# Two transformer layers on one core: the first 512 columns of each stage computed by tokens, between the two norms

## The chip, the core and the metric

The kernel runs on one core of a Trainium2 chip. The core has five engines with instruction queues of their own: TensorE (PE, with its weight loads shown as PEld), VectorE (DVE), ScalarE (ACT), GpSimd (POOL) and SyncE (SP), which here only issues DMAs. The metric is the device time of one launch in microseconds (us), the median of several runs; lower is better.

## The reference, cut to what matters

One sequence of 256 tokens and width 1024 goes through two layers, all in float32. Each layer is a mixer and a product-key expert layer, and each part begins with an RMS norm. Between the layers stands the first layer's final norm.

```
# layer 1
h    = rmsnorm(x, norm_mix_g);  proj = h @ w_in          # 3584 columns
       # retention (4 heads: q, k, v, gate) and differential attention (4 heads: q, k, v)
x    = x + concat([ret_out, diff_out]) @ w_out
x    = x + peer(rmsnorm(x, norm_ffn_g), wq, subkeys, u, v)
x    = rmsnorm(x, final_norm_g)
# layer 2
h    = rmsnorm(x, norm1);       proj = h @ w_in_2
       # gated delta rule (conv of q, k, v; a_gate) and HGRN2 (f, i, q, gate), two mixing gates
x    = x + mix @ w_out_2
x    = x + peer(rmsnorm(x, norm2), w_pq, sub_keys, expert_u, expert_v)
return rmsnorm(x, final_norm)

def peer(xn, wq, subkeys, u, v):     # 128*128 experts, 8 heads, 16 kept per head
    q = (xn @ wq)                    # 2048 columns: 8 heads x 2 halves x 128
    s = q . subkeys;  top 16 of each half, top 16 of their sums, softmax -> g
    act = gelu(u[e] . xn);  return sum(g * act * v[e])
```

## The kernel before

**Stages.** The program has four stages in a row: `mix1`, `Peer` 1, `mix2`, `Peer` 2, and the last norm (`final`). The 256 tokens are two tiles, `tt` = 0 and 1, of 128. Tokens lie on the partitions of `x`; the normed activations lie transposed, features on the partitions, as `xh` and `xl` (the fp32r-rounded value and what is left of it), 8 chunks of 128 features by 256 tokens.

**Weights.** Weights stream through in the order of a plan, 512 KB (128 x 1024 floats) at a time: `_dma` on SP's queue into a ring of three `raw` buffers, then `_conv` splits `raw` into `hi` (ACT, L159) and `lo` (L164, columns shared between DVE and POOL at `lo_cut`), in rings of three each. `prefetch(n)` issues conversions up to n weights ahead of use. `hold`, `homes` and the like don't exist yet.

**Tiles.** A weight of 128 output columns is used by `tile_ch` (L197): 8 chunks x 3 products (hi xh, hi xl, lo xh) = 24 matmuls of 256 tokens; output columns land on partitions, so a consumer that wants tokens there transposes. The results go to two `mm` banks in turn (in mix2 also `wm` banks). Output projections and the expert value rows go the other way: `acc_tile` (L278) keeps a chunk of activations as PE's weights and streams 512 columns of the weight row, into four `y` banks (two token tiles, two halves).

**Expert layer.** `Peer.run` makes 16 query tiles (`hp`, 8 heads x 2 halves); each starts a background `search` (scores, top 16). Then come 128 rows of u (U stage), and 128 rows of v (V stage). All experts are computed densely and the gates multiply them. The last `LAST` = 2 rows of v are held back: `acc_held` does both for token tile 0, then both for token tile 1, so that tile 0's sums are ready early.

**Seams.** After the last held row a norm starts: for each `tt`, `add_half` (L289 or L291) adds `y` to `x`, ACT squares and sums, DVE multiplies by the norm's weight (L370, in `norm_twice` L385 and L389), POOL takes the power -1/2 (L308), DVE builds a scaled identity (`diagonal`, L300), PE multiplies with it (L323, 16 records of 128 x 128 per token tile: transposes and scales), and ACT and DVE write `xh` (L325) and `xl` (L326). In program order both tiles' adds and transposes come first and the next stage's first `tile_ch` after them; this tile needs both token tiles. The first norm (`norm_first`, L342 to L354) needs no add.

**Order.** Each engine runs its queue in order. The queues are filled by a scheduler that simulates the program and by `issue_after`, which keeps one instruction behind another; background generators (`spawn`, `step`, `pass_round`) insert the attention, search and recurrence work between the weight tiles.

**mix1 and mix2.** `mix1` starts with four gate tiles (sigmoid on ACT, product `sg` L866 on DVE), then, per differential head, tiles q, k and v (v is transposed at L702 into `dv`), then retention. Between the gates and the first head the code computes the lambda of the differential attention on DVE (L742, L872, L874) from two small loads, `sub` and `dl`. `mix2` starts with 24 convolution tiles (three steps L1037 and a product L1049 each on DVE), between which `mix2_in_order` places 16 fillers: 8 `a_gate` tiles (L1454) and 8 `f` tiles. The delta rule's first half, `delta(0)`, needs the conv tiles of heads 0 to 3 and runs behind them.

Of the kernel before, what the change touches and what calls it, by code (L numbers as in the profile page):

```python
# [19 lines left out]
P = 128  # L20
# [64 lines left out]
class K:  # L85
    def __init__(self, tc, ins, ctx, plan):
# [16 lines left out]
        self.lo_cut = D  # L103
        self.uid = 0
# [80 lines left out]
    def tile_ch(self, xh=None, xl=None, tag=None):  # L185
# [13 lines left out]
        return ps  # L199

# [92 lines left out]

    def square(self, src, junk, acc):
# [19 lines left out]
    def transposed(self, tt, x, dr):  # L314
# [3 lines left out]
        for c4 in range(2):  # L318
            tag, ps = self.bank([P, 4, P])
            cs = slice(c4 * 4, c4 * 4 + 4)  # L320
            for c in range(4):
                cc = c4 * 4 + c
                nc.tensor.matmul(out=ps[:, c, :], lhsT=x[:, cc * P:(cc + 1) * P], rhs=dr, start=True, stop=True)  # L323
            h = self.xh[:, cs, ts]
            last = nc.scalar.activation(out=h, in_=ps, func=ACTF.Copy)  # L325
            nc.vector.tensor_tensor(out=self.xl[:, cs, ts], in0=ps, in1=h.bitcast(F32), op=ALU.subtract)  # L326
            self.done(tag)
        self.last_act = last.ins

    def prefetch_behind(self, ahead=3):  # L330

        with self.tc.issue_after(self.last_act):
            self.prefetch(ahead)

    def norm_first(self, g, xn):

        nc = self.nc
        banks = [self.bank([P, 2, 2, P]) for c2 in range(4)]
        for tt in range(2):
            x, s = self.x[:, tt, :], self.columns()  # L340
            self.square(x[:, 512:D], xn[tt][:, 512:D], s[0])
            nc.vector.scalar_tensor_tensor(out=xn[tt][:, 0:512], in0=x[:, 0:512], scalar=1.0 / D, in1=x[:, 0:512],  # L342
                                           op0=ALU.mult, op1=ALU.mult, accum_out=s[1])
            nc.vector.tensor_scalar(out=s[4], in0=s[0], scalar1=s[1], scalar2=EPS, op0=ALU.add, op1=ALU.add)
            self.rsqrt(s[6], s[4])
            dr = xn[tt][:, 0:P]
            self.diagonal(dr, s[6])
            for c in range(NC):
                nc.tensor.matmul(out=banks[c // 2][1][:, c % 2, tt, :], lhsT=x[:, c * P:(c + 1) * P], rhs=dr, start=True, stop=True)
        for c in range(NC):  # L350
            tag, ps = banks[c // 2]
            v, h = ps[:, c % 2].rearrange("p a b -> p (a b)"), self.xh[:, c, :]
            last = nc.scalar.activation(out=h, in_=v, func=ACTF.Copy, scale=g[:, c:c + 1])
            nc.vector.scalar_tensor_tensor(out=self.xl[:, c, :], in0=v, scalar=g[:, c:c + 1], in1=h.bitcast(F32),  # L354
                                           op0=ALU.mult, op1=ALU.subtract)
            if c % 2:
                self.done(tag)
# [555 lines left out]
H = 8  # L913
# [760 lines left out]
```

## Time and profile before

| | |
|---|---|
| time before, median of 3 runs | 2219.83 us (2218.16 to 2219.92) |
| the profiled execution | 2218.6 us |
| its span, first to last instruction | 2216.8 us |
| mean granted TensorE clock | 0.996 |
| PE busy | 2167.8 us, 98% |
| DVE, ACT, POOL busy | 1533.0, 1154.8, 813.5 us |

The span is 1.8 us shorter than the execution's own time. PE is busy in 98% of the span, so all idle time of PE together is 49 us (2216.8 less 2167.8). Rows begin with the start in us from the span's start, then the duration; "[2.38 <-DVE sg L866]" means that the engine stood idle for 2.38 us ahead of the instruction and that VectorE's instruction of line 866 ended this.

### The profile page before, as it was taken

Reading aid. Unit: us, or ns where it says so; the run is one execution under the profiler, and the core shown is the slowest. Engines: PE = TensorE matmul, PEld = TensorE weight load, DVE = VectorE, ACT = ScalarE, POOL = GpSimd, SP = SyncE. Lnnn points to the kernel's source line nnn. Section 1 sums busy time; section 2 is a strip of 40 time slices with the busy share of each in tenths; the row PEclk is TensorE's granted clock in tenths of the full one; section 3 lists DMA queues with packets and bytes.
Section 4 is the critical chain, followed back from the end, with each engine's and each line's share of the span. In section 5 each row is a group of like instructions: output and inputs, shape, how many; then the busy total and the mean of one; then the engine's idle time right before and its main releaser. Section 6 shows DMA issues by size and latency. Waiting matters only on the chain. (4 is left out here: it accounts for less than half of the span.)

```text
span 2216.8 us, 41395 instructions
## 1 busy us (share of the span) xinstructions
PE 2167.8 (98%) x15512; PEld 2016.0 (91%) x15512; DVE 1533.0 (69%) x3122; ACT 1154.8 (52%) x2183; POOL 813.5 (37%) x623
## 2 busy tenths in 40 slices
PE   8999999999999999989999999999999999999998
PEld 8989999999988888879899998999999999888887
DVE  5669986898644544477687787799778885444444
ACT  5645545444455555556455655455454445555554
POOL 3454000000065666646275675620000002665664
PEclk9999999999999999999999999999999999999999
DMA  5555655555556656534444244555555555665654
GB/s 188 155 176 162 185 170 167 157 162 161 172 190 207 200 192 196 193 118 137 131 123 135 68 143 152 173 162 185 178 162 158 157 160 183 193 206 190 195 194 152
DMA packets 103880, 370.89 MB, mean 167 GB/s; under 512 B 12928, under 2 KB 14080, under 8 KB 103424
## 3 DMA queue, kind: packets, MB, share of 16 engines
q1 hardware_dynamic: 101808, 365.21, 52.1%
q10 hardware_dynamic: 1872, 3.04, 0.5%
q8 instruction: 122, 2.00, 0.4%
q14 instruction: 78, 0.64, 0.1%
HBM read 367.16 MB, written 1.05 MB: 166 GB/s over the span
## 5 line engine op out<-in xcount | busy, mean ns | idle before, releaser
L164 POOL TENSOR_TENSOR lo<-raw,hi 128x384 fp32r<-128x384 f32 (+1 forms) x428 | 689.5, 1612 | 1309.1 <-ACT hi L159 1271.4
L159 ACT ACTIVATE hi<-raw 128x1024 fp32r<-128x1024 f32 x684 | 724.0, 1060 | 680.2 <-PE mm L197 403.4
L164 DVE TENSOR_TENSOR lo<-raw,hi 128x640 fp32r<-128x640 f32 (+1 forms) x654 | 668.0, 1022 | 313.5 <-ACT hi L159 306.2
L197 PE MATMUL mm<-xh,hi 128*128 128x256 f32 x2848 | 820.9, 288 | 4.4 <-DVE sg L866 2.9
L197 PE MATMUL mm<-xh,lo 128*128 128x256 f32 x2848 | 807.5, 284 | 0.3 <-DVE lo L164 0.2
L197 PE MATMUL mm<-xl,hi 128*128 128x256 f32 x2848 | 803.9, 282 | 0.9 <-DVE xl L326 0.7
L197 PEld LDWEIGHTS mm<-xh,hi 128*128 128x128 f32 x2848 | 538.2, 189 | 5.9 <-DVE sg L866 3.3
L197 PEld LDWEIGHTS mm<-xl,hi 128*128 128x128 f32 x2848 | 538.9, 189 | 1.8 <-DVE xl L326 1.1
L197 PEld LDWEIGHTS mm<-xh,lo 128*128 128x128 f32 x2848 | 534.8, 188 | 0.7 <-DVE lo L164 0.7
L278 PE MATMUL y<-lo,ah 128*128 128x512 f32 x1024 | 398.2, 389 | 0.0
L278 PE MATMUL y<-hi,ah 128*128 128x512 f32 x1024 | 397.4, 389 | 0.0
L278 PE MATMUL y<-hi,al 128*128 128x512 f32 x1024 | 275.9, 389 | 0.0
L635 DVE TENSOR_TENSOR al<-a,ah 128x256 fp32r<-128x256 f32 x256 | 118.1, 462 | 193.2 <-PE y L278 192.9
L278 PEld LDWEIGHTS y<-hi,al 128*128 128x128 f32 x1024 | 192.2, 188 | 39.9
L278 PEld LDWEIGHTS y<-lo,ah 128*128 128x128 f32 x1024 | 192.3, 188 | 39.8
L278 PEld LDWEIGHTS y<-hi,ah 128*128 128x128 f32 x1024 | 192.2, 188 | 39.8
L634 ACT ACTIVATE ah<-a 128x256 fp32r<-128x256 f32 x256 | 106.5, 417 | 168.3 <-PE y L278 166.7
L197 PE MATMUL wm<-xh,hi 128*128 128x256 f32 x320 | 92.1, 289 | 5.4 <-ACT sq L1059 2.1
L197 PE MATMUL wm<-xh,lo 128*128 128x256 f32 x320 | 90.6, 285 | 0.6 <-DVE lo L164 0.6
L197 PE MATMUL wm<-xl,hi 128*128 128x256 f32 x320 | 90.5, 283 | 0.3 <-DVE xl L326 0.3
L535 DVE TENSOR_TENSOR ow<-ow,w 128x1024 f16<-128x1024 f16 x128 | 87.1, 683 | 0.1
L563 ACT ACTIVATE a<-mm 128x256 f32<-128x256 f32 (+33 forms) x228 | 69.0, 302 | 0.0
(513 smaller groups left out, 2271.6 us busy)
## 6 DMA issues: line engine op xcount, KB each, us to landing
raw<-in_u_dram SPq DMA_DIRECT2D x256, 512.0 KB, 3.5
raw<-in_v_dram SPq DMA_DIRECT2D x256, 512.0 KB, 4.2
raw<-in_w_in_dram SPq DMA_DIRECT2D x108, 512.0 KB, 3.5
raw<-in_wq_dram SPq DMA_DIRECT2D x32, 512.0 KB, 3.7
raw<-in_w_out_dram SPq DMA_DIRECT2D x16, 512.0 KB, 3.6
raw<-in_w_branch_a_dram SPq DMA_DIRECT2D x8, 512.0 KB, 3.5
raw<-in_w_branch_b_dram SPq DMA_DIRECT2D x8, 512.0 KB, 3.6
skT<-in_sk_dram ACTq DMA_DIRECT2D x2, 1024.0 KB, 5.1
```

What stands on the lines that cost most here:

```text
L159: self.nc.scalar.activation(out=h, in_=r, func=ACTF.Copy)
L164: eng.tensor_tensor(out=l[:, a:b], in0=r[:, a:b], in1=h[:, a:b].bitcast(F32), op=ALU.subtract)
L197: self.nc.tensor.matmul(out=ps, lhsT=a[:, c, :], rhs=b, start=(c == 0 and k == 0), stop=(c == NC - 1 and k == 2))
L278: i = self.nc.tensor.matmul(out=self.y[tt][dh], lhsT=p[:, ts], rhs=q[:, ds], start=(first and m == 0), stop=(last and m == 2))
L535: nc.vector.tensor_tensor(out=ow[q], in0=ow[0], in1=some(self.w[:, q]), op=ALU.mult)
L563: nc.scalar.activation(out=a[:, s, n:T], in_=ps[:, n:T], func=ACTF.Gelu)
L634: nc.scalar.activation(out=h, in_=a, func=ACTF.Copy)
L635: nc.vector.tensor_tensor(out=l, in0=a, in1=h.bitcast(F32), op=ALU.subtract)
```

## The change

It has six parts.

1. **By tokens.** `tile_tok` and `seam` are new. The first 512 columns of each stage (mix1: the values of the four differential heads; both expert layers: queries hp 0 to 3; mix2: the first four `a_gate` heads) are no longer four `tile_ch` of 24 matmuls x 256, but 48 matmuls that stream 512 columns, 24 per token tile. Four weights in a new layout (`_quads`) hold them, each 2 chunks x 512 columns. In `seam`, three of four weights are used for tile 0 right after tile 0's transposes, ahead of tile 1's transposes (in mix1 two of them).
2. **Norm order.** `turn` and `behind` keep tile 1's first half of adds behind tile 0's scaled identity, and its second half behind tile 0's last `xl`. `xh` and `xl` are written in pairs of chunks from two banks in turn.
3. **Held rows.** `LAST` goes from 2 to 3. In the V stage a1's space is freed at n = 66, and the v rows converted from there on get homes of their own (`hold`, ring of four); `out_proj` and mix2's output do the same for their last weights, with deeper `prefetch`.
4. **mix1.** Values come token-major as `vt`: no v tile and no L702 transposes in `diff`. The lambda work moves into a generator behind the fourth gate.
5. **mix2.** Four a_gate fillers are gone, two fillers stand among the first 14 conv tiles (before: four among the first 12), then one behind each. `delta(0)` multiplies by the token-major gate `sgt` ahead of its transposes, and takes two banks at once.
6. **Expert layers.** The queries of hp 0 to 3 come from `qt` by two transposes each (8 per layer) and start at hp = 4, 7, 10, 13.

```
+    def tile_tok(self, tt, w, n, y):
+        h, l = w
+        ts = slice(tt * P, (tt + 1) * P)
+        todo = [(x, b, c2) for x, bs in ((self.xh, (h, l)), (self.xl, (h,))) for c2 in range(2) for b in bs]
+        for m, (x, b, c2) in enumerate(todo):
+            self.last_mm = self.nc.tensor.matmul(out=y, lhsT=x[:, 2 * n + c2, ts], rhs=b[:, c2 * 512:c2 * 512 + 512],
+                                                 start=(n == 0 and m == 0), stop=(n == 3 and m == len(todo) - 1)).ins
+
+    def seam(self, norms, before=3):
+
+        self.prefetch(2)
+        norms[0]()
+        with self.tc.issue_after(self.behind[0]):
+            self.prefetch(3)
+        ws = [self.weights() for _ in range(3)]
+        self.quads = [self.bank([P, 512])]
+        for n in range(3):
+            if n == before:
+                norms[1]()
+            self.tile_tok(0, ws[n], n, self.quads[0][1])
+        if before == 3:
+            norms[1]()
+        self.quads.append(self.bank([P, 512]))
+        for n in range(3):
+            self.tile_tok(1, ws[n], n, self.quads[1][1])
+            with self.tc.issue_after(self.last_act):
+                self.prefetch(n + 1)
+        w = self.weights()
+        for tt in range(2):
+            self.tile_tok(tt, w, 3, self.quads[tt][1])
...
+    def turn(self, tt, n):
+
+        return self.tc.issue_after(self.behind[n]) if tt else self.tc.issue_after(self.first_half) if n else nullcontext()
...
-            self.add_half(tt, dh, None)
-            self.square(x[:, hs], xn[:, hs], s[dh])
-        for dh in range(2):
-            hs = self.half(dh)
-            nc.vector.tensor_tensor(out=xg[:, hs], in0=x[:, hs], in1=gn[:, hs], op=ALU.mult)
+            with self.turn(tt, dh):
+                self.add_half(tt, dh, None)
+                self.square(x[:, hs], xn[:, hs], s[dh])
+                self.first_half = nc.vector.tensor_tensor(out=xg[:, hs], in0=x[:, hs], in1=gn[:, hs], op=ALU.mult).ins
...
-LAST = 2
+LAST = 3
...
-            for hp in range(16):
+            for hp in range(4, 16):
                 ps = k.tile_ch()
-                for gen in k.bg[:3]:
-                    pass
+                if hp % 3 == 1:
+                    k.spawn(search(hp // 3 - 1))
                 k.spawn(search(hp, ps))
...
+                    home = lambda: [end.tile([P, D], FR, name=t, tag=t, bufs=4) for t in ("wh", "wl")]
+                    k.hold(k.n_cv - k.n_use, [home] * (P - n - k.n_cv + k.n_use))
...
-                k.prefetch()
...
+                k.prefetch(2 if n < P - 20 else 3 if n < P - LAST - 1 else LAST + 2)
...
-    rest = [("a", h, 0) for h in range(H)] + [("f", h, 0) for h in range(H)]
+    rest = [("a", h, 0) for h in range(4, H)] + [("f", h, 0) for h in range(H)]
     for n, c in enumerate(conv):
         yield c
-        if n % 3 == 2 or n >= 12:
+        if n in (4, 9) or n >= 14:
             yield rest.pop(0)
```

What the scheduler makes of it shows in the engines' queues. First DVE at the start of mix1, before: `lo` is the weights' split, `sg` the gate product, L742 to L874 the lambda work (`sub`, `dl`).

```order
L164 TENSOR_TENSOR lo<-raw,hi 128x640 x3
L866 TENSOR_TENSOR sg<-mm,sig 128x256 x2
L164 TENSOR_TENSOR lo<-raw,hi 128x640
L742 TENSOR_SCALAR sub<-sub 128x1
L872 TENSOR_TENSOR pr<-dl 128x128
L874 TENSOR_REDUCE lam<-pr 128x2
L164 TENSOR_TENSOR lo<-raw,hi 128x640
L866 TENSOR_TENSOR sg<-mm,sig 128x256 x2
```

And DVE at the same place after the change (L167 is the split, L937 the gate product, L951 to L953 the lambda work):

```order
L167 TENSOR_TENSOR lo<-raw,hi 128x640 x5
L937 TENSOR_TENSOR sg<-mm,sig 128x256
L167 TENSOR_TENSOR lo<-raw,hi 128x640
L937 TENSOR_TENSOR sg<-mm,sig 128x256
L167 TENSOR_TENSOR lo<-raw,hi 128x640
L937 TENSOR_TENSOR sg<-mm,sig 128x256
L167 TENSOR_TENSOR lo<-raw,hi 128x640
L937 TENSOR_TENSOR sg<-mm,sig 128x256
L951 TENSOR_TENSOR pr<-dl 128x128
L953 TENSOR_SCALAR sub<-sub 128x1
L952 TENSOR_REDUCE lam<-pr 128x2
```

The three lambda instructions stood ahead of the third gate product, and now stand behind the fourth. Next DVE between `Peer` 1 and mix2, before: L291 adds, L385 and L389 multiply by two norm weights, L390 to L392 are small columns.

```order
L291 SCALAR_TENSOR_TENSOR x<-y,x 128x512 x2
L385 TENSOR_TENSOR a_4058<-x,a_4058 128x512
L389 TENSOR_TENSOR a_4058<-x,a_4058 128x512
...
L291 SCALAR_TENSOR_TENSOR x<-y,x 128x512
L390 TENSOR_SCALAR nrm<-nrm 128x1
...
L391 SCALAR_TENSOR_TENSOR nrm<-nrm 128x1
```

The same place after the change (L332 add, L433 and L435 the products, L345 the scaled identity, L375 `xl`):

```order
L435 TENSOR_TENSOR x_9411<-x,g_9408 128x512
L436 TENSOR_SCALAR nrm<-nrm 128x1
L437 SCALAR_TENSOR_TENSOR nrm<-nrm 128x1
L438 TENSOR_TENSOR nrm<-nrm 128x1
L345 TENSOR_SCALAR x_9412<-k_ident,nrm 128x128
L167 TENSOR_TENSOR lo<-raw,hi 128x640
L332 SCALAR_TENSOR_TENSOR x<-y,x 128x512
L433 TENSOR_TENSOR x_9413<-x,g_9406 128x512
L435 TENSOR_TENSOR x_9414<-x,g_9408 128x512
L375 TENSOR_TENSOR xl<-bg_10855,xh 128x2x128
```

Tile 0's chain down to its scaled identity has no instruction of tile 1 in it any more; one weight split stands between it and tile 1's first add. Last, PE at the same seam, before (L278 a held row, L323 transposes, L197 the first `tile_ch`):

```order
L278 MATMUL y<-hi,al 128x512
L323 MATMUL bg_10923<-a_4058 128x128 x4
L323 MATMUL bg_10930<-a_4058 128x128 x4
L323 MATMUL by_10953<-a_4058 128x128 x4
L323 MATMUL by_10960<-a_4058 128x128 x4
L197 MATMUL wm<-xh,hi 128x256
```

And after the change (L319 a held row, L370 transposes, L216 `tile_tok`):

```order
L319 MATMUL y<-wh,ow_10767 128x512
L370 MATMUL bg_10855<-x_9412,x_9411 128x128 x4
L370 MATMUL bg_10864<-x_9412,x_9411 128x128 x4
L216 MATMUL by_10880<-hi,xh 128x512
L216 MATMUL by_10880<-lo,xh 128x512
...
L216 MATMUL by_10880<-hi,xl 128x512 x2
L370 MATMUL by_10915<-x_9415,x_9414 128x128 x4
L370 MATMUL bg_10924<-x_9415,x_9414 128x128 x4
L216 MATMUL bg_10937<-hi,xh 128x512
```

Between the two tiles' transposes, which stood back to back, 18 matmuls of 512 columns now lie.

## Rows read from the trace of the kernel before

**Rows 1.** Of the page, part 1: each engine's busy time, share, instructions

```profile
PE 2167.8 (98%) x15512; PEld 2016.0 (91%) x15512; DVE 1533.0 (69%) x3122; ACT 1154.8 (52%) x2183; POOL 813.5 (37%) x623
```

**Rows 2.** The timeline at the start; columns: start, duration (both us), engine, line, operation

```profile
6.74 6.62 PE L349 MATMUL by<-xn,x 128*128 128x128 f32 x32 [6.74 <-DVE xn L300]
13.12 0.37 PE L197 MATMUL mm<-xh,hi 128*128 128x256 f32 x1
...
20.29 0.39 PE L197 MATMUL mm<-xh,hi 128*128 128x256 f32 x1 [0.55 <-DVE sg L866]
...
28.68 0.38 PE L197 MATMUL mm<-xh,hi 128*128 128x256 f32 x1 [2.38 <-DVE sg L866]
```

**Rows 3.** The timeline of DVE at the start

```profile
25.38 0.15 DVE L742 TENSOR_SCALAR sub<-sub 128x1 f32<-128x1 f32 x1 [2.28 <-DMA sub<-in_diff_subln_g_dram]
26.95 0.29 DVE L872 TENSOR_TENSOR pr<-dl 128x128 f32<-128x128 f32 x1 [1.41 <-DMA dl<-in_diff_lambda_dram]
```

**Rows 4.** Windows: us, busy time (x records) by engine, granted clock (PEclk), DMA share

```profile
29.00:33.00 4.00, 4.00 (x24) 4.00 (x23) 1.00 (x3) 1.06 (x1) 1.65 (x1) 0.59 0.56 195
955.00:957.00 2.00, 0.00 (x0) 0.00 (x0) 1.96 (x7) 1.31 (x4) 0.08 (x1) 0.50 0.00 0
974.00:984.00 10.00, 6.54 (x48) 5.56 (x48) 8.37 (x27) 6.77 (x20) 4.81 (x3) 1.00 0.34 109
1054.00:1064.00 10.00, 10.00 (x84) 9.81 (x83) 9.90 (x27) 6.36 (x17) 3.11 (x3) 1.00 0.69 200
```

**Rows 5.** The timeline of the first seam, mix1 to Peer 1

```profile
136.80 1.07 POOL L164 TENSOR_TENSOR lo<-raw,hi 128x384 fp32r<-128x384 f32 x1
...
136.93 1.63 DVE L164 TENSOR_TENSOR lo<-raw,hi 128x640 fp32r<-128x640 f32 x1
...
138.48 1.28 DVE L289 TENSOR_TENSOR x<-y,x 128x512 f32<-128x512 f32 x2
...
140.38 0.39 PE L278 MATMUL y<-hi,cl 128*128 128x512 f32 x1
...
143.22 2.02 PE L323 MATMUL bg<-xn,xg 128*128 128x128 f32 x16 [2.45 <-DVE xn L300]
...
147.55 0.39 PE L197 MATMUL mm<-xl,hi 128*128 128x256 f32 x1 [0.34 <-DVE xl L326]
...
147.78 0.28 PE L197 MATMUL mm<-xh,lo 128*128 128x256 f32 x1
...
150.65 0.29 PE L197 MATMUL mm<-xh,lo 128*128 128x256 f32 x1
```

**Rows 6.** The timeline of the second seam, Peer 1 to mix2

```profile
949.17 1.29 DVE L291 SCALAR_TENSOR_TENSOR x<-y,x 128x512 f32<-128x512 f32 x2 [0.30 <-PE y L278]
...
951.01 0.39 PE L278 MATMUL y<-lo,ah 128*128 128x512 f32 x1
...
951.69 0.39 PE L278 MATMUL y<-lo,ah 128*128 128x512 f32 x1
...
951.91 0.39 PE L278 MATMUL y<-hi,al 128*128 128x512 f32 x1
...
957.89 3.76 PE L323 MATMUL bg<-a 128*128 128x128 f32 x16 [5.59 <-issue]
...
963.95 0.39 PE L197 MATMUL wm<-xl,hi 128*128 128x256 f32 x1 [0.34 <-DVE xl L326]
```

**Rows 7.** The timeline of the third seam, mix2 to Peer 2

```profile
1398.45 0.39 PE L278 MATMUL y<-hi,ml 128*128 128x512 f32 x1
...
1404.94 0.39 PE L197 MATMUL mm<-xl,hi 128*128 128x256 f32 x1 [0.34 <-DVE xl L326]
```

**Rows 8.** DVE's groups by form in the first stretch of mix2, 964 to 1052

```profile
L164 DVE TENSOR_TENSOR lo<-raw,hi 128x640 fp32r<-128x640 f32 x22 | 21.3, 966 | 11.7 <-ACT hi L159 11.5
L1037 DVE SCALAR_TENSOR_TENSOR cva<-wm,i_conv_a,cva 128x255 f32<-128x255 f32 x14 | 6.7, 476 | 1.3 <-ACT cva L1035 1.3
...
L1049 DVE TENSOR_TENSOR qc<-cva,cvs 128x256 f32<-128x256 f32 x5 | 3.4, 688 | 0.8 <-ACT cvs L936 0.8
```

More of the change, by code (lines that the diff above doesn't have):

```diff
@@ L319, in transposed @@
             tag, ps = self.bank([P, 4, P])
-            cs = slice(c4 * 4, c4 * 4 + 4)
+            with self.tc.issue_after(self.last_mm) if tt else nullcontext():
+                for c in range(4):
+                    cc = c4 * 4 + c
+                    nc.tensor.matmul(out=ps[:, c, :], lhsT=x[:, cc * P:(cc + 1) * P], rhs=dr, start=True, stop=True)
+            for c in range(0, 4, 2):
+                cs = slice(c4 * 4 + c, c4 * 4 + c + 2)
+                h, v = self.xh[:, cs, ts], ps[:, c:c + 2]
+                last = nc.scalar.activation(out=h, in_=v, func=ACTF.Copy)
+                i = nc.vector.tensor_tensor(out=self.xl[:, cs, ts], in0=v, in1=h.bitcast(F32), op=ALU.subtract).ins
@@ new lines, in transposed, with norm_first @@
+            self.done(tag)
+        self.last_act = last.ins
+        self.behind[1] = i
+    def norm_first(self, tt, g, xn):
+        nc = self.nc
+        x, s = self.x[:, tt, :], self.columns()
+        self.square(x[:, 512:D], xn[:, 512:D], s[0])
+        nc.vector.scalar_tensor_tensor(out=xn[:, 0:512], in0=x[:, 0:512], scalar=1.0 / D, in1=x[:, 0:512],
+                                       op0=ALU.mult, op1=ALU.mult, accum_out=s[1])
+        nc.vector.tensor_scalar(out=s[4], in0=s[0], scalar1=s[1], scalar2=EPS, op0=ALU.add, op1=ALU.add)
+        self.rsqrt(s[6], s[4])
+        dr = xn[:, 0:P]
+        self.diagonal(dr, s[6])
+        ts = slice(tt * P, (tt + 1) * P)
+        for c4 in range(2):
+            tag, ps = self.bank([P, 4, P])
+            with self.tc.issue_after(self.last_mm) if tt else nullcontext():
+                for c in range(4):
+                    cc = c4 * 4 + c
+                    nc.tensor.matmul(out=ps[:, c, :], lhsT=x[:, cc * P:(cc + 1) * P], rhs=dr, start=True, stop=True)
@@ L335, in norm_first @@
[L335 to L357, printed above, removed]
@@ L412, in final @@
             hs = self.half(dh)
-            self.add_half(tt, dh, scale)
-            self.square(x[:, hs], xn[:, hs], s[dh])
-        for dh in range(2):
-            hs = self.half(dh)
-            nc.vector.tensor_tensor(out=xg[:, hs], in0=x[:, hs], in1=gb[:, hs], op=ALU.mult)
+            with self.turn(tt and not dh, dh):
+                self.add_half(tt, dh, scale)
+                self.square(x[:, hs], xn[:, hs], s[dh])
+                self.first_half = nc.vector.tensor_tensor(out=xg[:, hs], in0=x[:, hs], in1=gb[:, hs], op=ALU.mult).ins
         nc.vector.tensor_scalar(out=s[4], in0=s[0], scalar1=s[1], scalar2=EPS, op0=ALU.add, op1=ALU.add)
@@ L672, in run @@
                 k.step(BUD[1])
-                k.prefetch()
-            held = [(k.weights(), a) for a in last]
+                k.prefetch(2 if n < P - 20 else 3 if n < P - LAST - 1 else LAST + 2)
+            held = [(k.weights(), a) for a in parts]
             i = k.acc_held(0, held)
-            k.prefetch(1)
+            k.prefetch(2)
             with k.tc.issue_after(i):
                 k.acc_held(1, held)
-            for tt in range(2):
-                after(tt, 1.0 / GS, *gs, *(row(len(gs) + 3 * tt + m) for m in range(3)))
+            norms = [lambda tt=tt: after(tt, 1.0 / GS, *gs, *scratch[tt]) for tt in range(2)]
             if k.n_use < len(k.plan):
-                k.prefetch_behind()
+                k.seam(norms)
+            else:
+                for f in norms:
+                    f()
 CUT1 = 640
@@ L707, in transposed, with out_proj @@
     return v
-def out_proj(k, order, ch, cl, ready, last=2):
+def out_proj(k, order, ch, cl, ready, homes):
     wait = lambda: pass_round(k, 4)
     k.acc_begin(wait)
+    k.hold(len(order) - len(homes), homes)
     ws = []
@@ L1529, in run @@
                     k.acc_tile(tt, w, a, j == 0, False)
[L1530 removed]
+                k.prefetch(ahead)
             else:
```

221 lines of the change are left out of this document (137 added, 84 removed).

## The prediction

> **What bounds the kernel.** I read the page's busy shares first, then the waits of PE and the timelines around each, then windows. PE is busy for 2167.8 of 2216.8 us [rows 1]: matrix work sets the time, and all that scheduling can win is the 49 us of idle PE, plus what changes in the work itself. The timelines say where such idle lies in places that the change touches: the start [rows 2], three seams [rows 5 to 7], and mix2's first stretch [rows 4]. In each the reader should look at the last wait in brackets.
>
> **Pace.** In [rows 5] the same product of a `tile_ch` recurs from 147.78 to 150.65: a tile of 24 matmuls costs 2.87 us, 0.1196 each. In [rows 6] three 512-column matmuls take 951.69 less 951.01, so 0.227 each. Four tiles of 96 matmuls cost 11.48; 48 wide ones cost 10.90. The width alone gives 0.58 per stage, 2.3 us over four stages; it is contained in the terms below.
>
> The Trainium skill, "TensorE: Matmul & The Clock Gate", section "Wait — 56ns, not 53.3ns?", has a warm matmul start every N/2.4 GHz plus about 2.5 ns. By it two narrow ones lose only some 2.7 ns to a wide one, 0.5 us over the 192 pairs, and the forecast would be 1.8 us later. The rows show both widths some 10 ns slower than the page, and the measurement decides.
>
> **Part 1 and 4, the start.** Before, tile 0 starts at 13.12 and the fifth tile at 28.68, after 2.38 idle: four tiles occupy PE until 26.3 [rows 2]. After: tile 0's transposes are 16 of the 32 records that took 6.62, so 3.3, to 10.05. Then 12 wide matmuls, between 2.7 at 0.227 and 5.4 at twice that (the transposes ran slowly here, 0.207 each against 2.02/16 = 0.126 in [rows 5]); I take 4.1, to 14.2. Tile 1's transposes 2.0, then 36 wide ones 8.2: 24.4. That is 1.9 earlier. The 0.55 wait for the gate product at 20.29, which with its restart costs about 0.8, can come back at the gates, so I count 1.1.
>
> The 2.38 is a chain: the third gate product waits on DVE behind L742 and L872, which wait 2.28 and 1.41 for two small loads [rows 3]. Behind the fourth gate nothing that PE waits for soon stands after them but the splits, and the loads are asked for ahead of the four gate tiles, 11.5 us of PE's work earlier. I count 2.4. Right behind this wait, 29 to 33, the granted clock is 0.59, close to the lower of two levels, 1.2 GHz [rows 4]: 4 x 0.41 = 1.6 lost, and gone if PE doesn't stand idle. Sum of the start: 5.1; bounds 2 (a new wait of equal kind) and 6.
>
> Values by tokens need no transposes: 8 fewer, at the 0.126 of [rows 5], +1.0. The differential heads then come every two tiles, 5.7 us, instead of three, 8.6, with the same DVE work per head. Background work can spill into the retention tiles; I take -0.7, bounds -3 and 0.
>
> **Part 2 and 3, the seams.** "E" is the end of the last held matmul's pace. Before the change, from E to the first tile's running start (one narrow matmul ahead of the last wait shown), plus four tiles:
> - seam 1: E = 140.38 + 0.23 = 140.61, to 147.43: 6.8 + 11.5 = 18.3 [rows 5]
> - seam 2: E = 952.14, to 963.83: 11.7 + 11.5 = 23.2 [rows 6]
> - seam 3: E = 1398.68, to 1404.82: 6.1 + 11.5 = 17.6 [rows 7].
>
> After, seam 1. Tile 0's sums are ready 12 matmuls ahead of E, -2.7. Two adds and two products on DVE at 0.64 (1.28 for two, [rows 5]) end at -0.15; ACT's last square 0.2 later; column work, POOL's power and the diagonal some 1.4 more: transposes at about E + 1.5, 2.0 long. Then 18 wide matmuls, 4.1: PE has work to E + 7.7. Tile 1 on DVE, from the diagonal at 1.1: a split (0.8 to 1.6), add and product 1.3, four `xl` 1.7, add and product 1.3, then 0.5 for the square and 1.4 as above: transposes at 8.5, to 10.5. So 0.8 idle; then 18 matmuls and 12, to 17.5. Gain 0.8. Seam 3 has the same instructions: 17.4, gain 0.2.
>
> Seam 2 has two more norm products (three DVE operations per half). Before, its first add starts at 949.17, E - 3.0 [rows 6]; a third held row gives six matmuls more, so E - 4.3. Six DVE operations and the rest of the chain put transposes at E + 0.9. PE has work to 7.1. Tile 1's chain: split 1.6, three products 1.9, `xl` 1.7, three more 1.9, squares, columns and POOL 1.7: transposes at 9.5, after 2.4 idle, to 11.5; 30 wide ones to 18.4. Gain 4.8. Before, PE stood idle for 5.59 and then ran 16 records in 3.76 instead of 2.02: the clock was 0.50, 1.2 GHz, in 955 to 957 [rows 4, 6]. Whether 2.4 idle brings that again is open: after 2.45 in seam 1 it didn't [rows 5], after 2.38 at the start it did [rows 2, 4]. Price 1.6, not taken into the sum.
>
> Deeper prefetch and homes lie beside V rows that PE is saturated by; cost 0. Without that cover a split late by its own 0.8 shows once per stage.
>
> **Part 5, mix2.** One conv tile costs DVE a split 0.97, three steps of 0.476 and a product 0.5 to 0.69 [rows 8], about 2.95, as much as PE's 2.87; a filler costs about 1.45. Before, the first 16 tiles load DVE with 12 x 2.95 + 4 x 1.45 = 41.2 of PE's 45.9; after, 14 x 2.95 + 2 x 1.45, plus two wide products for `sgt` (1.4), 45.6. So the slack falls from 4.7 to 0.3, and DVE has other work there: 8.37 of 10 in 974 to 984, where PE idles 3.46, and 9.90 in 1054 to 1064, where PE has none idle [rows 4]. Bounds: all of the lost slack and one tile of delay for `delta(0)` behind it, -8; or waits such as the 3.46 go away, +3. I take -2, since later splits come earlier by four a_gate tiles, and the conv tiles are through four tiles sooner.
>
> **Part 6.** 16 transposes over two expert layers, 0.126 each: -2.0. The searches' tail lies under the U rows, on engines that PE does not wait for; cost 0, and a wait would show at the gates' end.
>
> **The tail** has the same operations in another order; an add moved is 0.64 either way, 0 taken.
>
> **Sum.** 5.1 + 1.0 - 0.7 + 0.8 + 4.8 + 0.2 - 2.0 - 2.0 = 7.2. The profiled execution, 2218.6, becomes 2211.4; the median lies 1.2 above it, so 2212.6. I say 2212.
>
> **Rivals.**
> - mix2 gives more back: -8 instead of -2. Then 1.2 is left: 2218.6, no change. For it: DVE at 9.90 of 10 in 1054 to 1064. Against it: PE has no idle time in that same window.
> - Slower: conv tiles paced by DVE. Each of the 14 early conv tiles pays 0.75 (a POOL overlap stretching one split and one product), 10.5, and `delta(0)` ends two tiles, 5.7, later against the remaining work. That is 16.2 against the 9.2 won elsewhere: 2226.8. It decides from 13.6 up, with 4.4 as the bound of "slower".
> - A split holds up each norm chain. In [rows 5] a split of DVE takes 1.63 when it starts 0.13 after POOL's 1.07 long one, against a mean of 0.97 in [rows 8]. At two places per seam, 0.7 each, three seams: 4.2 lost, 2216.8. The Trainium skill, "SBUF — State Buffer", section "SBUF: two separate sides", has DVE operations with two SBUF inputs and GpSimd take turns on one locked port; the row agrees. That rule speaks against splits packed around the norms.
> - The start finds another wait: gates wait for their splits, since after the four token-major weights DVE has five splits to catch up. The 2.4 and 1.6 return: 2216.6.
> - Better: mix2's waits shrink, +3: 2207.6.
>
> **How the numbers follow.** What a measurement tells from no change is about 0.2%, 4.4 us: faster is below 2215.4. My case gets 0.46; better 0.12; a norm or start rival in part, still below 2215.4, 0.12; one of them whole, or mix2's -8: 0.19, within 0.2%; slower 0.11. So 0.70, 0.19, 0.11. From 2204 (better, with no loss in the diff phase and the start's upper bound) to 2219 (mix2's whole price) no more than 2 in 10 is left out. The likeliest case alone has 2208 to 2215.
>
> **What would show it.** The fourth gate product follows the third without a load in between, and PE has no gap above 1 us from 14 to 45, with granted clock 1.00 throughout. At each seam, wide matmuls stand between the two tiles' transposes; idle of 0.5 to 1 (seams 1, 3) and about 2.4 (seam 2) ahead of the second; no 0.50 clock. From the second seam's E to the first conv tile: 18.4. Wrong would be: PE's idle time from 964 on up by more than 6 us with DVE as releaser, or waits of PE for `hi` or `lo` in the wide matmuls, or a search or gate wait at the U rows' end.

## The result, and the profile after

The changed kernel takes 2238.5 us (6 runs, 2236.55 to 2239.58), before 2220.24 us (6 runs beside it): ratio 1.0082, 95% interval 1.0069 to 1.0095. It is 18 us slower, 0.8%, where 8 us faster was forecast. The page, engines' busy time, to be held against [rows 1]:

```profile
span 2237.8 us, 41013 instructions
...
PE 2179.2 (97%) x15328; PEld 2009.8 (90%) x15328; DVE 1536.1 (69%) x3152; ACT 1158.3 (52%) x2195; POOL 810.1 (36%) x621
```

The span is 21.0 us longer. PE has fewer instructions and is busy 11 us longer: part of its work ran slower. To see where, both traces are cut at the same ten places, and a window is read for each stretch. The cuts are starts of PE instructions: the first and the last output-row matmul of each block (0.23 added to the last), the first narrow matmul behind the second seam, and the first matmul of `delta`'s solve (`X,decc`). So, in order, the stretches are mix1, its output rows, Peer 1 up to V, V, second seam, conv tiles up to the solve, the rest of mix2, its output rows, Peer 2 up to V, V. Columns: stretch, us, busy us of PE, PEld, DVE, ACT, POOL, granted clock, DMA share, GB/s. Before:

```profile
0.00:112.70 112.70, 102.53 (x798) 100.76 (x799) 66.39 (x122) 64.88 (x148) 45.53 (x41) 0.98 0.55 172
112.70:140.61 27.91, 27.91 (x144) 23.20 (x142) 15.23 (x21) 12.61 (x25) 13.09 (x10) 1.00 0.58 172
140.61:603.97 463.36, 460.28 (x4072) 456.62 (x4071) 386.64 (x889) 226.83 (x469) 40.46 (x19) 1.00 0.54 168
603.97:952.14 348.17, 348.17 (x1538) 288.11 (x1536) 169.38 (x259) 188.65 (x259) 211.36 (x128) 1.00 0.61 196
952.14:963.23 11.09, 5.50 (x34) 5.37 (x33) 7.00 (x19) 5.33 (x13) 4.31 (x6) 0.69 0.05 21
963.23:1080.59 117.36, 107.44 (x876) 103.81 (x875) 97.66 (x209) 69.35 (x152) 57.98 (x48) 1.00 0.48 147
1080.59:1362.60 282.01, 271.23 (x2241) 261.57 (x2241) 210.55 (x420) 154.21 (x365) 171.89 (x213) 0.99 0.36 113
1362.60:1398.68 36.08, 36.08 (x216) 31.70 (x214) 26.45 (x38) 16.26 (x22) 18.99 (x13) 1.00 0.67 200
1398.68:1861.33 462.65, 460.28 (x4071) 456.62 (x4071) 386.15 (x888) 226.84 (x469) 40.42 (x19) 1.00 0.54 167
1861.33:2209.51 348.18, 348.18 (x1538) 288.21 (x1536) 164.49 (x258) 187.12 (x256) 208.42 (x126) 1.00 0.58 189
```

And after:

```profile
0.00:111.54 111.54, 102.08 (x773) 98.05 (x773) 63.91 (x131) 66.87 (x153) 52.08 (x42) 1.00 0.56 178
111.54:137.36 25.82, 24.87 (x114) 19.59 (x112) 16.03 (x22) 13.10 (x25) 14.41 (x11) 1.00 0.67 204
137.36:599.54 462.18, 460.80 (x4031) 454.76 (x4031) 388.06 (x894) 225.95 (x471) 34.62 (x17) 1.00 0.53 166
599.54:953.84 354.30, 351.64 (x1538) 289.25 (x1536) 172.01 (x262) 190.76 (x262) 213.81 (x130) 1.00 0.60 195
953.84:970.60 16.76, 14.13 (x75) 11.36 (x75) 11.55 (x28) 8.93 (x22) 8.92 (x13) 1.00 0.27 76
970.60:1090.06 119.46, 105.65 (x814) 102.01 (x812) 90.42 (x199) 66.02 (x146) 55.48 (x41) 0.94 0.43 133
1090.06:1372.44 282.38, 269.98 (x2212) 259.08 (x2213) 210.07 (x425) 152.74 (x362) 166.09 (x209) 0.99 0.35 111
1372.44:1412.28 39.84, 36.91 (x216) 31.48 (x214) 27.93 (x39) 18.37 (x24) 21.11 (x15) 1.00 0.66 199
1412.28:1875.93 463.65, 461.31 (x4032) 454.94 (x4031) 387.92 (x894) 225.74 (x471) 34.63 (x17) 1.00 0.53 166
1875.93:2230.37 354.44, 351.64 (x1538) 289.26 (x1536) 165.12 (x260) 187.58 (x257) 208.37 (x127) 1.00 0.57 186
```

Read the second column of each pair. mix1 with its output rows is 3.2 us shorter, Peer 1 up to V 1.2 shorter, Peer 2 up to V 1.0 longer. The loss is in three places: each V stage is 6.1 to 6.3 longer; seam and conv stretch of mix2 together take 136.2 instead of 128.4, 7.8 longer; mix2's output rows take 3.8 longer.

**The V stage.** The timeline of ACT at row 66, where the weights' places change from the ring (`hi`) to homes (`wh`); `ah` are the activations that PE needs for a row:

```profile
775.65 0.42 ACT L695 ACTIVATE ah<-a 128x256 fp32r<-128x256 f32 x1 [0.70 <-PE y L319]
778.17 1.06 ACT L163 ACTIVATE wh<-raw 128x1024 fp32r<-128x1024 f32 x1 [2.11 <-DMA raw<-in_v_dram]
779.14 1.04 ACT L163 ACTIVATE hi<-raw 128x1024 fp32r<-128x1024 f32 x1
780.08 0.40 ACT L695 ACTIVATE ah<-a 128x256 fp32r<-128x256 f32 x1
780.90 1.07 ACT L163 ACTIVATE wh<-raw 128x1024 fp32r<-128x1024 f32 x1 [0.41 <-DMA raw<-in_v_dram]
785.92 1.06 ACT L163 ACTIVATE wh<-raw 128x1024 fp32r<-128x1024 f32 x1 [3.96 <-DMA raw<-in_v_dram]
786.88 0.70 ACT L695 ACTIVATE ah<-a 128x256 fp32r<-128x256 f32 x2
```

Before the change a conversion waits for PE to be done with a place in the ring, and so falls between two `ah`; at the same row there:

```profile
780.07 0.42 ACT L634 ACTIVATE ah<-a 128x256 fp32r<-128x256 f32 x1 [0.70 <-PE y L278]
781.03 1.06 ACT L159 ACTIVATE hi<-raw 128x1024 fp32r<-128x1024 f32 x1 [0.54 <-PE y L278]
```

After it, a `wh` waits for its row's load alone. The first `wh` stands ahead of the `hi` of the row before it, and two more `wh` stand ahead of two `ah`. The last of them waits 3.96 us for its row's load, and the `ah` behind it comes late. PE's timeline there:

```profile
787.33 0.50 PE L319 MATMUL y<-wh,ah 128*128 128x512 f32 x1 [2.66 <-ACT ah L695]
```

And the windows behind it (granted clock third from the end):

```profile
788.00:790.00 2.00, 2.00 (x8) 1.57 (x7) 2.00 (x2) 0.30 (x1) 2.00 (x2) 0.69 1.01 385
790.00:792.00 2.00, 2.00 (x6) 1.52 (x6) 2.00 (x2) 1.33 (x3) 2.00 (x2) 0.50 0.71 238
792.00:794.00 2.00, 2.00 (x10) 1.67 (x9) 2.00 (x2) 0.99 (x2) 1.42 (x2) 0.96 0.06 23
```

From 788 to 794 the clock falls to 0.50, 1.2 GHz, and costs 2 x (0.31 + 0.50 + 0.04) = 1.7 us. A wait of 2.66 costs 4.4. The remaining 1.7 us of each V stage are in PE's own pace (see the end).

**mix2.** At the second seam PE waits 1.46 and 1.17 us ahead of the two tiles' transposes, where [rows 6] had 5.59; there the change works as it was meant to:

```profile
955.47 2.02 PE L370 MATMUL bg<-x,x 128*128 128x128 f32 x16 [1.46 <-DVE x L345]
963.10 1.16 PE L370 MATMUL by<-x,x 128*128 128x128 f32 x8 [1.17 <-DVE x L345]
```

In the conv stretch behind it PE stands idle 119.46 - 105.65 = 13.8 us instead of 9.9, with single waits up to 3.06, and the mean clock is 0.94, some 7 us lost. Two of the waits:

```profile
986.75 0.69 PE L1130 MATMUL bg<-k_ident,qc 128*128 128x128 f32 x2 [2.78 <-DVE qc L1125]
1017.26 0.44 PE L206 MATMUL wm<-xh,hi 128*128 128x256 f32 x1 [3.06 <-ACT vs L1138]
```

In the output rows PE waits 0.97 and 1.88 us; ahead of the `mh` that ends the second, ACT has a conversion of the next stage's weight, which itself waits for its load:

```profile
1406.24 1.06 ACT L163 ACTIVATE hi<-raw 128x1024 fp32r<-128x1024 f32 x1 [0.75 <-DMA raw<-in_wq_dram]
1407.99 1.19 PE L319 MATMUL y<-oal,mh 128*128 128x512 f32 x4 [1.88 <-ACT mh L1627]
```

### The profile page after: what moved, and what is told of

It reads as the page before. It is cut to its first block, busy times and chain, and to the rows that moved or that the text cites. A ratio compares the mean times of both kernels' runs of the same rounds, so it can differ in the third digit from the quotient of the medians.

```text
span 2237.8 us, 41013 instructions
## 1 busy us (share of the span) xinstructions
PE 2179.2 (97%) x15328; PEld 2009.8 (90%) x15328; DVE 1536.1 (69%) x3152; ACT 1158.3 (52%) x2195; POOL 810.1 (36%) x621
## 5 line engine op out<-in xcount | busy, mean ns | idle before, releaser
L163 ACT ACTIVATE hi<-raw 128x1024 fp32r<-128x1024 f32 x555 | 587.8, 1059 | 614.4 <-PE mm L206 388.6
L167 POOL TENSOR_TENSOR lo<-raw,hi 128x384 fp32r<-128x384 f32 (+1 forms) x299 | 478.0, 1601 | 1180.3 <-ACT hi L163 1142.4
L167 DVE TENSOR_TENSOR lo<-raw,hi 128x640 fp32r<-128x640 f32 (+1 forms) x531 | 562.8, 1060 | 222.3 <-ACT hi L163 214.2
L167 POOL TENSOR_TENSOR wl<-raw,wh 128x384 fp32r<-128x384 f32 x125 | 205.1, 1641 | 138.9 <-ACT wh L163 138.9
L319 PE MATMUL y<-hi,ah 128*128 128x512 f32 x544 | 210.7, 389 | 0.0
L319 PE MATMUL y<-lo,ah 128*128 128x512 f32 x544 | 210.6, 389 | 0.0
L319 PE MATMUL y<-wh,ah 128*128 128x512 f32 x464 | 182.7, 394 | 5.5 <-ACT ah L695 5.5
L319 PE MATMUL y<-wl,ah 128*128 128x512 f32 x464 | 182.4, 393 | 0.0
L163 ACT ACTIVATE wh<-raw 128x1024 fp32r<-128x1024 f32 x125 | 132.4, 1059 | 84.0 <-PE y L319 61.8
L167 DVE TENSOR_TENSOR wl<-raw,wh 128x640 fp32r<-128x640 f32 x125 | 106.6, 853 | 85.5 <-ACT wh L163 85.4
L319 PE MATMUL y<-hi,al 128*128 128x512 f32 x544 | 145.4, 389 | 0.0
L319 PE MATMUL y<-wh,al 128*128 128x512 f32 x464 | 127.9, 396 | 0.0
L319 PEld LDWEIGHTS y<-hi,al 128*128 128x128 f32 x544 | 102.1, 188 | 21.2
L319 PEld LDWEIGHTS y<-lo,ah 128*128 128x128 f32 x544 | 102.1, 188 | 21.1
```

Source lines behind the costliest of these rows:

```text
L167: eng.tensor_tensor(out=l[:, a:b], in0=r[:, a:b], in1=h[:, a:b].bitcast(F32), op=ALU.subtract)
L319: i = self.nc.tensor.matmul(out=self.y[tt][dh], lhsT=p[:, ts], rhs=q[:, ds], start=(first and m == 0), stop=(last and m == 2))
```

## The experiments

All ran on one core like the kernel itself. The times are medians of 4 to 12 runs, the ratio is to the kernel before in runs beside it. Lengths of single stretches come from one profiled execution each.

| run | us | ratio, 95% interval |
|---|---|---|
| the changed kernel | 2238.5 | 1.0082, 1.0069 to 1.0095 |
| e1_homes_late | 2233.6 | 1.0059, 1.0042 to 1.0076 |
| e2_homes_in_turn | 2231.0 | 1.0052, 1.0035 to 1.0068 |
| e3_fillers_back | 2235.5 | 1.0064, 1.0047 to 1.0081 |
| e4_out_ring | 2236.0 | 1.0062, 1.0045 to 1.0079 |
| e5_v_in_turn | 2229.3 | 1.0046, 1.0029 to 1.0063 |
| e6_mix2_tiles | 2239.4 | 1.0079, 1.0060 to 1.0098 |
| e7_spare_tiles | 2236.3 | 1.0067, 1.0051 to 1.0084 |
| e8_lambda_early | 2242.3 | 1.0104, 1.0079 to 1.0128 |
| e9_mix2_before | 2220.7 | 1.0001, 0.9992 to 1.0010 |
| e10_one_bank | 2232.7 | 1.0052, 1.0037 to 1.0067 |
| e11_best | 2220.2 | 1.0002, 0.9992 to 1.0011 |
| e12_v_before | 2223.2 | 1.0013, 1.0003 to 1.0023 |
| e13_home_pairs | 2228.8 | 1.0041, 1.0029 to 1.0053 |
| e14_old_norms_2 | 2219.7 | 0.9998, 0.9989 to 1.0007 |
| e15_late_old_norms_2 | 2218.1 | 0.9989, 0.9979 to 0.9998 |

**The V stages: e1, e2, e5, e13.** e1 holds later, e2 keeps the conversions in order:

```
+                if n == P - LAST - 6:                      # e1
                     k.hold(k.n_cv - k.n_use, [home] * (P - n - k.n_cv + k.n_use))
...
+        with self.tc.issue_after(self.last_hi) if placed else nullcontext():      # e2
+            self.last_hi = self.nc.scalar.activation(out=h, in_=r, func=ACTF.Copy).ins
```

> In both V stages the weights go into homes of their own only from row 119 on, not from row 66; the pool change and the loads of the norm weights stay at row 66. Theory A (ACT's order at the change from ring to homes: three conversions stand ahead of activations that PE needs) keeps the wait and the half clock behind it and moves them to about row 119, since the order there has the same shape; only the slower pace of home rows goes, 53 rows x 0.027 us x 2 = 2.9 us: about 2235.6 us. Theory B (the norm weights' loads at row 66 delay the rows' loads) has no home waiting there, so the stall of 2.7 us and the half clock of 1.7 us are gone in both stages: about 2238.5 - 8.8 - 2.9 = 2226.8 us.

The waits of 2.7 at row 66 are gone, in their place come 0.8 and 1.2 us near row 119 in the first V stage and 1.2 in the second, without a fall of the clock. The V stages take 351.9 and 350.1 us. So neither theory is whole. At the wait of 1.2 too a conversion that waits for its load (4.18 us, mix2's first weight) stands ahead of the `ah`: the order makes the wait, and how late the load comes sets its size. That the norm weights' loads are what makes it 2.7 at row 66 was not tested by itself.

> As the changed kernel, but each conversion into a home is kept behind the conversion ahead of it on ACT, so that at the change from ring to homes ACT's queue alternates again: one conversion, one activation. Theory A: the wait of 2.7 us at row 66 and the half clock of 1.7 us behind it go in both V stages, each 354.1 to 349.7 us long: about 2238.5 - 8.8 = 2229.7 us. Theory B (the norm weights' loads): the stall stays, as the loads stand where they stood: 2238.5 us.

ACT's timeline at the same place alternates, `ah` comes in time although its conversions still wait for loads, and PE has no idle time in the whole stage (busy 349.79 of 349.79):

```profile
778.23 1.06 ACT L165 ACTIVATE hi<-raw 128x1024 fp32r<-128x1024 f32 x1 [0.54 <-PE y L321]
779.79 1.07 ACT L165 ACTIVATE wh<-raw 128x1024 fp32r<-128x1024 f32 x1 [0.50 <-DMA raw<-in_v_dram]
780.75 0.41 ACT L697 ACTIVATE ah<-a 128x256 fp32r<-128x256 f32 x1
782.47 1.06 ACT L165 ACTIVATE wh<-raw 128x1024 fp32r<-128x1024 f32 x1 [1.31 <-DMA raw<-in_v_dram]
783.44 0.40 ACT L697 ACTIVATE ah<-a 128x256 fp32r<-128x256 f32 x1
```

Theory A holds: without the wrong order the loads cost nothing. The median fell by 7.5, not 8.8; mix1's output rows, whose homes were kept in turn too, took 29.2 instead of 25.8. In mix2's output rows the turn did not help, the block takes 40.0.

e5 is e2 with the order kept in the V stages alone (`if placed and self.in_turn`, set at `hold` and cleared behind the last row).

> As the changed kernel, but in the two V stages alone each conversion into a home is kept behind the conversion ahead of it; the output rows of mix1 and mix2 stay free. Theory A: both V stages 349.8 instead of 354.3 us and no granted clock below 1.00 in them, mix1's output block 25.8 us again (29.2 where all homes were kept in turn): about 2238.5 - 9.0 = 2229.5 us. Rival (the V stages' clock loss comes back elsewhere): 2233 us or more.

2229.3 as expected; V 350.0 and 349.8, mix1's output rows 25.8. The changeover costs 9.2 us of the 18 by the medians, 8.9 by the lengths of the two stages.

e13 puts both halves of a home side by side: `w = end.tile([P, 2, D], ...)`, `w[:, 0, :], w[:, 1, :]`.

> As e5 (V homes in turn), but the two halves of a home, wh and wl, lie side by side (4 KB apart) instead of in two rings (16 KB apart). Theory F (the distance of the two rows that PE streams in turn sets 0.227 or 0.229 us a matmul): home rows fall to 2.720 us, each V stage from 349.8 to 348.2, about 2229.3 - 3.2 = 2226 us. Rival (it is where the homes lie as a whole, or the bank of what is written beside them): 2.747 us a row stays, 2229.3 us.

V stays at 349.8, the rival holds. Why a home's rows run slower is open.

**mix2's output rows: e4.** The two `hold` lines and the deeper `prefetch` of mix2's end are taken out (`ahead = 2`).

> As the changed kernel, but mix2's output rows use the ring of three as before, converted two ahead: no homes in the places of the gates and decays. Theory A (deep conversions ahead of activations on ACT make PE wait, 1.0 and 1.9 us at 1404 and 1406, ACT mh and DVE ml late): the output block takes 36 us instead of 39.6: about 2234.9 us. Rival (the block is longer because mix2's background work ends later): 39.6 stays, 2238.5 us.

The block takes 36.1 again, PE without idle time, as theory A says. The total fell by 2.5 only: the way to the block was 2.6 us longer in the profiled run, with clock losses at other waits. The homes there and the deeper `prefetch`, which e4 doesn't separate, cost 3.7.

**mix2's first stretch: e3, e7, e6, e10, e9.**

```
-        if n in (4, 9) or n >= 14:                         # e3
+        if n in (2, 5, 8, 11) or n >= 16:
```

> As the changed kernel, but mix2 places its 12 fillers nearly as before: one behind every third of the first 12 conv tiles (four), then one behind each of the last eight. Theory C (two fillers in place of four leave PE without cover at the start of mix2): the gaps of 2.8 and 3.1 us at 984 and 1014 and the half clock behind them go, and from the second seam to the output rows PE takes 410 us instead of 418.6: about 2230 us. Rival (the token-major gate, its sigmoid and its products on ACT and DVE in front of the first conv tiles make the gaps): 2238.5 us within 2, with the first gap still near 984.

The gap at 984 stays at 2.8, the one at 1014 goes, others of 2.1, 1.35 and 1.35 come at 1060 to 1084. The stretch from the first conv tile to the solve takes 120.5, and from the last held row to the output rows it is 416.2, where theory C said 410. Theory C is wrong: moving fillers moves waits.

e7 adds `k.spare()` behind four conv tiles, which repeats the tile's 24 matmuls.

> As the changed kernel, with four more tiles of 24 matmuls in mix2's conv stretch (behind conv tiles 2, 7, 9 and 12; each repeats the conv tile ahead of it on the same weight into another bank, read by nobody), 11.5 us more of PE work and none for DVE, ACT or DMA. Theory D: from the first conv tile to delta's first solve it takes 119.5 us within 3, as the work replaces idle and half-clock time; 2238.5 us within 4. Rival (PE's work sets that stretch, and its waits come on top): 131 us there, 2250 us.

The windows of its seam and conv stretch:

```profile
953.58:972.50 18.92, 15.74 (x76) 13.04 (x76) 12.24 (x30) 9.54 (x24) 8.92 (x13) 0.91 0.25 74
972.50:1090.02 117.52, 113.81 (x931) 111.94 (x930) 95.07 (x202) 66.97 (x147) 55.23 (x41) 0.99 0.45 140
```

With 11.5 us more of PE's work the stretch is 2 us shorter and the seam ahead of it 2 us longer: 136.4 together, 136.2 without. Idle time in the stretch falls from 13.8 to 3.7 and the clock from 0.94 rises to 0.99. As theory D says for this run, the work replaces idle and half-clock time and is free.

That a chain outside of PE sets the length, as e6's text below has it for theory D, doesn't follow, and the traces speak against it. e2 has the same conv stretch as the changed kernel:

```profile
967.65:1083.97 116.32, 102.99 (x814) 99.30 (x812) 91.15 (x199) 65.83 (x146) 54.20 (x41) 0.97 0.44 137
```

It is 3.1 us shorter at a clock of 0.97 instead of 0.94, and a chain outside of PE would not feel PE's clock. By the clock's own records the changed kernel, e1, e2, e4, e5, e8, e10 and e13 lose 3.4 to 6.8 us there, and less this loss their stretches are 112.3 to 113.9 long. The kernels whose conv stretch is that of before (before, e9, e11, e12, e14, e15) lose 0 to 4.4, and less this loss have 115.7 to 117.4. So, as far as these show, taking out the four tiles wins some 3 us, far less than their 11.5, and the falls of the clock take that back.

e6 goes back to tiles for all a_gate heads (plan, `rest`, `delta`'s gate as before, no `seam` at Peer 1's end), on top of e5.

> As e5, and mix2 computes all eight a_gate heads by tiles of 24 matmuls, with the order of conv tiles and fillers of before; at the second seam both norms run one after the other without token-major work between them. Theory D (the stretch from the first conv tile to delta's first solve lasts 117 us whatever PE does in it, since a chain over DVE and ACT sets it; the token-major gate only takes PE work out of it and starts it later): the stretch stays 116 to 120 us, the way from the seam to the first conv tile falls from 16.8 to 8 to 11 us, and the idle and half-clock time in the stretch falls from 20.6 to about 10: about 2229.5 - 7 = 2222.5 us. Rival (mix2's loss comes from the other edits there, both banks at once in delta and the output homes): 2229.5 us or more.

It was 10 us slower than e5 instead of 7 faster:

```profile
962.93:1085.17 122.24, 109.61 (x874) 106.36 (x873) 96.10 (x211) 66.82 (x145) 58.69 (x46) 0.97 0.44 136
1085.17:1378.99 293.82, 280.14 (x2244) 267.72 (x2243) 208.70 (x418) 157.57 (x372) 174.52 (x213) 0.97 0.35 108
```

The seam fell to 12.2, but the conv stretch got no shorter, and behind the solve 11.2 us more than in e5 were lost, 6.8 of them to the clock (0.97 instead of 0.99). So something else in mix2 costs too.

```
-            yield from k.need(2)                           # e10, e9
-            banks = [k.bank([P, 4, P]) for tt in range(2)]
+            for tt in range(2):
+                yield from k.need(1)
+                bt, ps = k.bank([P, 4, P])
```

> As the changed kernel, but delta takes one bank at a time as before, instead of two at once. Theory E (both banks at once cost time in mix2): from the second seam's end to the output rows 412 to 414 us instead of 418.6, about 2233 us. Theory D (the token-major gate ahead of the first conv tile is the whole loss, 7.8 us up to the first solve, and nothing behind it): 418.6 within 2, 2238.5 us.

From the last held row to the output rows 415.2 instead of 418.6, half of what theory E said; 2232.7. In this run's profile the V waits of 2.6 and 2.8 us brought no fall of the clock, so a part of the 5.8 us is not mix2's. And the 415.2 shows little: with mix2 unchanged up to the output rows, e1, e2, e4, e5, e8 and e13 have 415.9 to 421.2.

> As e6 (V homes in turn, all a_gate heads by tiles, old order of conv tiles and fillers), and in mix2 also delta with one bank at a time, the gate's wait where it was, and the output rows in the ring of three: mix2 is then the kernel's of before, but for the order of the norms at its two ends. Theory E (the two banks taken at once cost e6 its 9 us from the first to the last solve): from the second seam's end to mix2's output rows 411 to 413 us (before 410.5, e6 428.3), the output block 36 us: about 2229.3 - 6.5 - 3.7 = 2219 us. Rival (something outside of mix2, the norms' order or the pools behind Peer 1, slows it): 420 us or more there, 2228 us or more.

2220.7, 8.6 less than e5: from the last held row to the output rows 412.1, output rows 36.1. With mix2 and the V order as before, the loss is gone. From e6 to e9 16 us go up to the output rows, with the banks and the place of one wait changed there; no run has one of the two without the other, and what the banks are worth with the new fillers (3.4 us in e10's profile) is not clear of the spread.

**The lambda work: e8** (back at its old place in the program).

> As the changed kernel, but the lambda work stands at its old place in the program, ahead of the first head; the scheduler now puts it ahead of the first gate product on DVE. If it is what made the 2.4 us wait of before, PE waits about as long at the gates again, with half clock behind it: mix1 up to its output rows takes 111.5 + 4 = 115.5 us, 2242.5 us. Rival (the loads have landed by then, since the token-major weights go first; the wait that is left at 30.7, 1.35 us, is the gate's own chain): 111.5 us, 2238.5 us.

The total is the expected one, but not by the expected way. PE's wait at the gates is 2.88 us instead of 1.35, yet the clock stays at 1.00, and mix1 up to its output rows takes 112.5, only 0.9 longer than after. The rest of the span's 4.2 us is mostly a second V stage of 357.6, 3.1 longer, whose code the edit leaves as it was: its home rows run slower still (see the end). So the lambda work does hold up the gates, by 1.5 us; what that is worth in mix1's length can't be told, since the kernels without this edit, with the same mix1, have 111.1 to 113.0 there.

**Versions: e11, e12, e14, e15.** e11 is e9 with e1's late homes. e12 has the V stages as before (`LAST = 2`, no homes). e14 and e15 are e12 and e11 with the old order of the norms at the second seam (`if True:` for `with self.turn(tt, dh):` in `norm_twice`).

> As e9, and the V rows go into homes only from row 119 on, in turn. What is left of the change are the token-major columns of mix1 and of both expert layers, the norms' order, three held rows and mix1's output homes. If the ring's rows keep 0.227 us a matmul up to row 119, each V stage takes 348.4 instead of 349.9 us: about 2219 - 3 = 2216 us, faster than before by 0.2%. Rival (the late change from ring to homes makes waits of 0.8 and 1.2 us again, as it did without the conversions in turn): 2219 us, no change from before.

> As e9 (mix2 as before), and the V stages as before too: two held rows, no homes, two weights ahead; the pool change at row 66 stays. What is left of the change is mix1, the token-major queries and the norms' order. From the stretches measured apart: mix1 137.8 instead of 140.6, from there to V 462.1 instead of 463.4, V 348.2, mix2 411 instead of 410.5 and 36.1, Peer 2 up to V 463.6 instead of 462.7, V 348.2: about 2217 us, 3 us below before. Rival (the loads at row 66 make a wait in V even without homes): 2220 us or more.

e12's V stages are 348.2, but the second seam grows:

```profile
947.87:964.17 16.30, 6.92 (x34) 6.52 (x33) 9.91 (x23) 7.04 (x19) 5.47 (x7) 0.75 0.14 48
```

> As e12, but at the second seam alone both tiles' adds and products interleave on DVE as before. If the order of the norms makes that seam long, the way from its end to the first conv tile falls from 16.3 to 11 to 12 us, with one wait of some 5.6 us instead of 4.0 and 5.4: about 2223.2 - 5 = 2218 us; with less half clock behind it down to 2216 us. Rival (the seam is long because of the two held rows alone): 2223 us.

> As e11 (three held rows, homes from row 119 on, in turn), with the old order of the norms at the second seam. If the third held row moves the adds 1.4 us ahead, the seam takes 9.5 to 10.5 us instead of 12.0: about 2220.2 - 2 = 2218 us. Rival (the V stages' late homes and the seam's gain cancel, and the half clock behind the wait decides): 2220 us.

```profile
950.22:959.17 8.95, 5.28 (x33) 5.12 (x32) 5.67 (x17) 4.63 (x13) 4.72 (x6) 0.81 0.01 2
959.17:1078.23 119.06, 109.63 (x876) 106.47 (x874) 95.99 (x211) 69.16 (x153) 57.88 (x47) 0.97 0.47 140
```

e14's seam takes 11.7, so tile 0 first, then tile 1, without work between, costs 4.6 us: two waits, 4.0 and 5.4, where e14 has one of 6.4. In e15, with the third held row, the seam takes 9.0. e15 is the fastest, 2218.1, 0.9989 of before with an interval that just excludes 1, and less than the 0.2% taken here as the bound. e11 and e12 missed by 4 and 6 us: in e11 the change to homes at row 119 still makes waits in the first V stage, 350.9 instead of 348.4, as its rival said, and in e12 the seam took 16.3. The conv stretch lasts 117 to 120 in all of them, and clock losses of 0.5 to 4.4 us in it come and go.

## Why the prediction was wrong

**The step that failed first** is one sentence: "Deeper prefetch and homes lie beside V rows that PE is saturated by; cost 0." PE had no idle time there, but ACT feeds it row by row, and a home takes away the wait for PE that kept ACT's conversions behind its activations. What that costs is shown by e2 and e5: 9.2 us. Home rows' pace adds 1.6 per stage, and the same edit in mix2's output rows 3.7 (e4). Together about 16 of the 21 us of span. A term was put at nothing because the engine that bounds the stage was full; the order in the queue of an engine with time to spare was not asked for.

**The second** is part 5 together with seam 2. The seam's 4.8 and mix2's -2 were added as if independent, and the 4.8 holds the four a_gate tiles' 11.5 us as if each us of PE's work taken out of the conv stretch shortened it. Seam 2 came out better than worked out (16.8 to the first conv tile, 18.4 expected). But the conv stretch, at 117.4 before, should have gone to 117.4 - 11.5 + 2 = 107.9, and took 119.5. PE's busy time without the clock's loss fell by 8.6 us there; idle time rose by 3.9, and falls of the clock cost 6.8. The windows of before had a sign: 9.9 us of PE idle in the conv stretch and 3.46 in 974 to 984 [rows 4], with DVE's load worked out as equal to PE's. Seam and stretch went from 128.4 to 136.2 where 123.6 + 2 was expected: 10.6 us off, beyond the bound of -8 on mix2. The rival "slower: conv tiles paced by DVE" named the place; its price of 0.75 for each conv tile is not what happened, since the stretch itself grew by 2 only, and DVE is busy for 90.4 of its 119.5 us. The waits end with results of DVE and of ACT; which chain of them PE waits for was not taken apart.

**The clock.** I asked whether the 2.4 us at seam 2 would bring half speed back and left out waits elsewhere. Seam 2 stayed at 1.00, with waits of 1.46 and 1.17 and none of 2.4; but new waits of 2.0 to 3.1 us in V and in the conv stretch were followed by stretches of 0.50: 3.4 us lost in both V stages, some 7 in the conv stretch. It isn't certain: the wait of 2.65 ahead of the solve was followed by none, and behind the solve 3.4 were lost after waits of 1.65 and less. The Trainium skill, "TensorE: Matmul & The Clock Gate", section "HAM oscillation — how this bites in real kernels", has a kernel whose matmuls wait for data between bursts, so that the clock falls in the wait and the next burst starts slow, each time anew. The trace of the V stages agrees, with 2.66 us of wait and 1.7 lost, though the fall begins behind the wait's end (0.69 from 788 to 790); e10, with 2.55 and nothing lost, shows that it needn't come.

**What was right.** Seam 1's and 3's mechanism (waits of 1.1 instead of 2.5 and 1.8; Peer 1 up to V -1.2 where +0.2 was summed, Peer 2 +1.0 where +0.8 was; the second is luck in part, as the same Peer 2 takes 460.7 to 464.2 in the other runs). mix1 gained 3.2 instead of 5.4: clock 1.00 throughout as forecast, but the gate product still makes PE wait 1.35, a gap above the 1 us that was named as the sign, and `xh` 0.26 and 0.54 at the first wide matmuls. e8 shows that the lambda work would still have held up the gates, by 1.5 us more.

## What to carry to other kernels

Ask of every stretch what sets its length before giving or taking work: an engine that stands idle inside a stretch gains little from losing work there, since its idle time grows and its clock may fall, and it can take more for nothing (e7: 11.5 us). A buffer that need not be waited for also removes an order: keep the order of conversions and activations that the wait gave, or the queue of the engine may serve the far future first. A wait of 2 to 3 us on PE should be priced with up to 1.7 us more, since the clock may fall behind it.

## What the runs showed of the hardware that was not expected

Rows streamed from homes run at 2.747 us for 12 matmuls, rows from the ring at 2.720: with no idle time a V stage with homes in its last 60 rows takes 349.8 us, without 348.2. Halves side by side or in two rings make no difference (e13). The pace of homes is not one value either: in the second V stage of e8, with 2.78 us idle and 1.7 lost to the clock, the home rows take 2.80 us, and this alone makes that stage 3.1 us longer. Why is open. And waits of 2.5 to 3.0 us at the same row of V brought a slower clock in both stages of the changed kernel, e3, e4, e7 and e8, and in neither of e10, whose V stages have the same code.
